# Layer 0's feed-forward network: up projection by a seven-product scheme, activations through DRAM, down projection as one stage

## The chip, the cores and the metric

One core of a Trainium2 chip runs the whole program; the other seven cores are idle. The metric is the device time of one execution in microseconds (us). PE is the matrix engine, PEld its weight loads, DVE the vector engine, ACT the scalar engine, POOL the GpSimd engine and SP the queue that issues nearly all transfers. L292 means line 292 of the kernel before; in rows of the changed kernel the numbers are those of its own file.

## The reference, cut to what matters

Two layers of a block; each has token mixers and then a feed-forward network. In layer 0 it runs over 768 tokens (512 of x, 256 of context), in layer 1 over the 512 of x. D is 1024, D_FF is 2816, all in float32.

```python
def dwconv3(x, w):                      # along tokens, x and context apart
    xp = jnp.pad(x, ((0, 0), (1, 1), (0, 0)))
    return xp[:, :-2] * w[0] + xp[:, 1:-1] * w[1] + xp[:, 2:] * w[2]

def conv_ffn(u, w_up, w_conv, w_down):
    a = dwconv3(u @ w_up, w_conv)       # w_up [1024, 5632]
    gate, val = jnp.split(a, 2, axis=-1)
    return (jax.nn.silu(gate) * val) @ w_down   # w_down [2816, 1024]

fx = conv_ffn(modulate(rmsnorm(x, g), shift, scale), ffn_up[l], ffn_conv[l], ffn_down[l])
x = x + mod_x[5] * rmsnorm(fx, norm_g[l, 3])
```

## The kernel before

**Numbers in two parts.** Each float32 factor is split into a high part that the matrix engine takes exactly and a low rest. A product is three passes: high by high, high by low, low by high. The input of the up projection lies in SBUF as UH and UL, features on the partitions. A weight tile is loaded (`load`, L262, on SP), ACT casts the high part (L255) and POOL subtracts it from the raw tile to get the low part (L256, `wl`, 128x1024). Both subtraction inputs lie in SBUF.

**Up projection of layer 0.** The 5632 columns are 22 pairs of 128-wide tiles, a gate tile f and a value tile f. `fm` (L305 and on) computes one tile for all 768 tokens: 8 k-tiles, three passes, and for each a matmul of 512 and one of 256 columns (L292), so 48 matmuls a tile and 96 a pair. The first pair goes through `fms`, which cuts the tokens into pieces of 256 and also computes the gate tile of pair 1.

**After a pair** (`up_pair`, L1286 and on) the three-tap convolution runs straight from PSUM: ACT scales the middle tap into `fcv` (L552), DVE adds the two others (L554, L557) for 512 and 256 tokens. Then ACT's Silu (L1298), DVE's product (L1299), ACT's high part `ah` (L1302) and DVE's low part `al` (L1303).

```python
    def dwconv(dst, src, w, hc):        # src is a place in PSUM
        ACT.activation(dst[:, 0:n], src[:, 0:n], AF.Copy, scale=w[1])
        for a, b in ((0, TX),) + (((TX, T),) if hc else ()):
            DVE.scalar_tensor_tensor(dst[:, a + 1 : b], src[:, a : b - 1], w[0], dst[:, a + 1 : b], ...)
            DVE.scalar_tensor_tensor(dst[:, a : b - 1], src[:, a + 1 : b], w[2], dst[:, a : b - 1], ...)
```

**Down projection of layer 0** (`ffn`, L1319 and on) is mixed in between: after each group of 2 to 5 pairs (`EDGES`), `down` (L1306; its products L1311) multiplies the group's activations with its rows of w_down for each of the six 128-token tiles j, and the result is added to y[j] in SBUF: ACT copies the first group (L1337), DVE adds the others from PSUM (L1339). In all 792 matmuls of 512 columns. The last group ends in `residual` (norm, gain, residual sum) and `to_u`, which transposes the result on PE into the input of layer 1.

**Beside it** `mod_dve` computes layer 1's six modulation vectors: w_mod comes in 512 KB pieces, DVE keeps a running sum `macc` (L416, L418; 128x512, all in SBUF), and ACT, POOL (L428, `ml`) and PE finish each half.

**What sets the order.** The program text is not the order of an engine: a scheduler lays the instructions of each engine out at build time by priorities and an estimate of durations. At run time each engine takes its own list strictly in that order and waits at its head. Tiles in PSUM (`mm` twice, `b2` once, two `b1`) and weight buffers (5 raw, 3 high) are given out in program order.

Of the kernel before, what the change touches and what calls it, by code (L numbers as in the profile page):

```python
# [44 lines left out]
def block_kernel(  # L45
# [412 lines left out]
    def mod_first(ch, hf, md):  # L458
        """Half of the columns of a chunk of layer 0, summed on DVE."""
# [19 lines left out]
    def mod_pe(ch, hf, md):  # L479
        """The same on PE."""  # L480
# [10 lines left out]
    def square(np_, ss, src):  # L491
        """ss = the mean square of src over the D features, or its part from these."""
# [10 lines left out]
    def to_u(np_, l, which, j0, xns, ks=range(KC)):  # L503
        """Modulate normalized token tiles j0, ... into the input of the next products."""
# [4 lines left out]
        for k in ks:  # L509
            ps = b1()  # L510
            for i, xn in enumerate(xns):
                PE.transpose(ps[:, i * P : (i + 1) * P], xn[:, k * P : (k + 1) * P], ident)
            tt = np_.tile([P, n], F32, tag="tt", name=nm("tt"), bufs=3)
            ACT.activation(
                tt, ps[:, 0:n], AF.Identity, scale=a[:, k, part : part + 1], bias=b[:, k, part : part + 1]
            )
            DVE.tensor_copy(UH[:, k, o : o + n], tt)  # L517
            DVE.tensor_sub(UL[:, k, o : o + n], tt, UH[:, k, o : o + n].bitcast(F32))  # L518
# [10 lines left out]
    def residual(np_, gs, j, y, src, v, dst, last):  # L529
        """v = x + mod * rmsnorm(y) for token tile j, stored; unless last, normalized again in place."""  # L530
# [30 lines left out]
    # ================= mLSTM gates =================  # L561
    def gate_prep(l, gp, cols):
# [32 lines left out]
        # rows 0-3: forward, in processing order (context, then x); rows 32-35: backward, reversed  # L595
# [31 lines left out]
        def natural(dst, src, fn):  # L627
            """dst (x then context, natural order) = fn(src) (processing order)."""
# [459 lines left out]
    def run(*gens):  # L1088
        """Round robin: (generator, steps per round)."""
# [16 lines left out]
    # ================= the layers =================  # L1106
# [5 lines left out]
    # first norm and first modulation  # L1112
# [51 lines left out]
    for l in range(2):  # L1164
# [62 lines left out]
        def rows(wr, w, k, bufs, eng=POOL):  # L1227
            raw, _ = load(w[k * P : (k + 1) * P, :].unsqueeze(1), 1)
            h = wr.tile([P, 1024], F32R, tag="wrh", name=nm("wrh"), bufs=bufs)
            lo = wr.tile([P, 1024], F32R, tag="wrl", name=nm("wrl"), bufs=bufs)  # L1230
            ACT.copy(h, raw)  # L1231
            eng.tensor_sub(lo, raw, h.bitcast(F32))  # L1232
            return h, lo

# [20 lines left out]
        y = [t(yb, [P, D], f"y{j}") for j in range(njs)]  # L1255
# [3 lines left out]
        for j in range(njs):  # L1259
# [14 lines left out]
            if j % 2:  # L1274
                late = to_u(np_, l, 1, j - 1, y[j - 1 : j + 1])
# [4 lines left out]
        if l == 1:  # L1280
            more_slots(raw=4)
# [37 lines left out]
        def ffn():  # L1319
            edges = EDGES[l]  # L1320
            pairs = [up_pair(0)]
            for g in range(len(edges) - 1):
# [4 lines left out]
                ws = [rows(wr, ffn_down[l], f, DOWN_ROWS[l]) for f in range(lo, hi)]  # L1327
# [15 lines left out]
        if l == 0:  # L1343
            pcs[1] = params(1, nc.sync)
            up = ffn()
            for _ in range(2):
                next(up)
            run((up, 1), (seq(*[mod_dve(1, ch, fp) for ch in (1, 0, 2, 4, 3, 5)]), 1))
        else:
            run((ffn(), 1))  # L1350
# [6 lines left out]
        for j in range(DOWN_AHEAD[l]):  # L1357
            pss.append(next(ring)())
            down(av, ws, j, pss[j], 0, len(av) - 1)
        for j in range(njs):  # L1360
            end = j == njs - 1
            if j < DOWN_AHEAD[l]:
# [8 lines left out]
            dst = x2d[j * P : (j + 1) * P, :] if l == 0 else out[0, j * P : (j + 1) * P, :]  # L1371
            residual(np_, gs, j, y[j], x1d[j * P : (j + 1) * P, :], y[j], dst, l == 1)
            if l == 0 and j % 2:
                late = to_u(np_, 1, 0, j - 1, y[j - 1 : j + 1])
        if l == 0:
            def ending(np_, yb, late):
                yield from late
                np_.release()
                yb.release()

            late = ending(np_, yb, late)
            wr.release()
            np_.release("gt0", "gt1", "xr", "sq")
            yb.release(*[f"y{j}" for j in range(4)])
            continue
# [84 lines left out]
```

## Time and profile before

| what | value |
|---|---|
| time of the 3 runs | median 2684.73 us (2673.37 to 2686.26) |
| profiled execution, first to last instruction | 2676.3 us (the page gives no other time of this execution) |
| median of the runs above that span | 8.4 us |
| mean granted clock of PE | 0.994 |
| chain of waits that ended last | PE 31% of the span, DVE 3%, all others under 2% |
| transfers | 297.96 MB, mean 111 GB/s |
| busiest lines on POOL | L256 637.0 us and L1232 118.0 us, both the low parts of weights |

Busy shares of an engine include the time in which it holds an instruction that cannot start yet. The mean over the span mixes stages, so the feed-forward stage of layer 0 is read by itself: its first product starts at 1022.4 us (L292 after the last w_out product) and the first product of layer 1 starts at 1605.6 us.

### The profile page before, as it was taken

What the parts mean: (1) busy time and instruction counts of PE and PEld (TensorE: products, weight loads), DVE (VectorE), ACT (ScalarE), POOL (GpSimd) and SP (SyncE); (2) the same over time, 40 slices, a digit from 0 to 9 for tenths busy, and PEclk for the clock granted to TensorE, in tenths of its full rate; (3) what the DMA queues carried; (4) which work ended last, traced back from release to release, by engine and by line L of the source; (5) the groups of instructions that cost most, each with busy time, mean ns of one, the idle gap of its engine ahead of it and who ended that gap; (6) DMA issues with size and microseconds to landing.
All of it is one profiled execution on the core that took longest, in us unless ns stands there. A gap on an engine that the chain in (4) does not pass through costs nothing. (4 is left out here: it accounts for less than half of the span.)

```text
span 2676.3 us, 35623 instructions
## 1 busy us (share of the span) xinstructions
PE 2583.5 (97%) x13859; PEld 2169.5 (81%) x13859; DVE 1449.0 (54%) x2510; ACT 992.0 (37%) x1663; POOL 896.2 (33%) x522
## 2 busy tenths in 40 slices
PE   6999999999999999999999999999999998999998
PEld 2887888888888878888888878787888876888886
DVE  6688784332462456477665565665434646523334
ACT  3454553222222234323322345555232333543332
POOL 3222223333232223233332333323343433444432
PEclk9999999999999999999999999999999999999999
DMA  6334353321331443233433342323433436433321
GB/s 230 91 110 126 104 162 117 113 79 56 106 96 57 132 138 120 88 110 119 134 119 102 121 137 84 109 82 117 126 103 101 120 96 189 150 95 95 99 67 55
DMA packets 321267, 297.96 MB, mean 111 GB/s; under 512 B 12532, under 2 KB 264252, under 8 KB 321100
## 3 DMA queue, kind: packets, MB, share of 16 engines
q1 hardware_dynamic: 320184, 294.11, 35.8%
q8 instruction: 110, 1.80, 0.3%
q10 hardware_dynamic: 916, 1.58, 0.2%
q14 instruction: 57, 0.47, 0.1%
HBM read 269.30 MB, written 26.35 MB: 110 GB/s over the span
## 5 line engine op out<-in xcount | busy, mean ns | idle before, releaser
L256 POOL TENSOR_TENSOR wl<-raw,wh 128x1024 fp32r<-128x1024 f32 x260 | 637.0, 2452 | 1198.6 <-ACT wh L255 1152.1
L292 PE MATMUL mm<-UH,wh 128*128 128x512 f32 (+1 forms) x2248 | 657.3, 352 | 6.8 <-DVE UH L517 4.6
L292 PE MATMUL mm<-UL,wh 128*128 128x512 f32 (+1 forms) x2248 | 645.3, 348 | 1.8 <-DVE UL L518 1.8
L255 ACT CAST wh<-raw 128x1024 fp32r<-128x1024 f32 x260 | 272.6, 1049 | 540.3 <-PE mm L292 363.0
L292 PE MATMUL mm<-UH,wl 128*128 128x512 f32 (+1 forms) x2248 | 451.6, 348 | 0.0
L292 PEld LDWEIGHTS mm<-UH,wh 128*128 128x128 f32 x2248 | 368.1, 189 | 63.7 <-DVE UH L517 5.7
L292 PEld LDWEIGHTS mm<-UL,wh 128*128 128x128 f32 x2248 | 366.5, 189 | 57.7 <-DVE UL L518 2.2
L292 PEld LDWEIGHTS mm<-UH,wl 128*128 128x128 f32 x2248 | 358.2, 189 | 56.3 <-issue 3.2
L418 DVE SCALAR_TENSOR_TENSOR macc<-mraw,sc,macc 128x512 f32<-128x512 f32 x224 | 206.4, 946 | 19.4 <-DMA mraw<-in_w_mod_dram 18.4
L1232 POOL TENSOR_TENSOR wrl<-raw,wrh 128x1024 fp32r<-128x1024 f32 x48 | 118.0, 2471 | 167.0 <-ACT wrh L1231 125.8
L292 PE MATMUL mm<-ys,wh 128*128 128x512 f32 (+1 forms) x768 | 166.0, 361 | 7.7 <-DVE bth L1020 7.1
L292 PEld LDWEIGHTS mm<-ys,wh 128*128 128x128 f32 x768 | 124.8, 188 | 30.2 <-issue 4.8
L554 DVE SCALAR_TENSOR_TENSOR fcv<-mm,fcol,fcv 128x511 f32<-128x511 f32 x89 | 58.3, 655 | 139.6 <-ACT fcv L552 139.5
L1231 ACT CAST wrh<-raw 128x1024 fp32r<-128x1024 f32 x60 | 62.7, 1050 | 140.7 <-DMA raw<-in_ffn_down_dram 63.9
L292 PE MATMUL mm<-U,wh 128*128 128x512 f32 (+1 forms) x496 | 111.2, 376 | 0.2 <-DVE y L536 0.2
L292 PEld LDWEIGHTS mm<-U,wh 128*128 128x128 f32 x496 | 89.2, 188 | 17.4 <-DVE y L536 0.4
L1020 DVE SCALAR_TENSOR_TENSOR bth<-bth,mm 128x768 f32<-128x768 f32 (+1 forms) x48 | 39.2, 817 | 115.6 <-PE mm L292 108.5
L1311 PE MATMUL mm<-wrh,ah 128*128 128x512 f32 x302 | 95.5, 393 | 1.2 <-DVE fcv L557 1.2
L1311 PE MATMUL mm<-wrl,ah 128*128 128x512 f32 x302 | 95.5, 393 | 0.0
L1311 PE MATMUL mm<-wrh,al 128*128 128x512 f32 x302 | 95.4, 392 | 0.0
L292 PE MATMUL mm<-ys,wl 128*128 128x512 f32 (+1 forms) x384 | 85.3, 357 | 0.0
L554 DVE SCALAR_TENSOR_TENSOR cv<-mm,pcol,cv 128x511 f32<-128x511 f32 (+1 forms) x28 | 17.7, 632 | 118.6 <-ACT cv L552 118.6
(306 smaller groups left out, 4116.2 us busy)
## 6 DMA issues: line engine op xcount, KB each, us to landing
raw<-in_w_in_dram SPq DMA_DIRECT2D x140, 512.0 KB
mraw<-in_w_mod_dram SPq DMA_DIRECT2D x88, 512.0 KB
raw<-in_ffn_up_dram SPq DMA_DIRECT2D x88, 512.0 KB
raw<-in_ffn_down_dram SPq DMA_DIRECT2D x44, 512.0 KB
raw<-in_w_branch_dram SPq DMA_DIRECT2D x32, 512.0 KB
gates<-bth SPq DMA_DIRECT2D x24, 384.0 KB
bth<-gates SPq DMA_DIRECT2D x24, 384.0 KB
raw<-in_w_out_dram SPq DMA_DIRECT2D x16, 512.0 KB
```

The source lines that it names most:

```text
L255: ACT.copy(h, raw)
L256: POOL.tensor_sub(lo, raw, h.bitcast(F32))
L292: PE.matmul(ps[:, c0:c1], lhsT=lw, rhs=r, start=s, stop=e)
L418: DVE.scalar_tensor_tensor(acc[v], mr[:, kk], sc[:, k, v : v + 1], acc[v], op0=ALU.mult, op1=ALU.add)
L554: DVE.scalar_tensor_tensor(dst[:, a + 1 : b], src[:, a : b - 1], w[0], dst[:, a + 1 : b], op0=ALU.mult, op1=ALU.add)
L1020: DVE.scalar_tensor_tensor(th[:, 0:n], th[:, 0:n], 1.0, pb[:, 0:n], op0=ALU.add, op1=ALU.mult)
L1231: ACT.copy(h, raw)
L1232: eng.tensor_sub(lo, raw, h.bitcast(F32))
L1311: PE.matmul(ps[:, h], lhsT=av[i][q][:, j * P : (j + 1) * P], rhs=ws[i][r][:, h], start=pi == 0 and i == 0, stop=pi == 2 and i == len(av) - 1,)
```

## The change

It touches layer 0's feed-forward network alone. Layer 1 keeps the old scheme.

- **Up by seven products.** Pairs 0 and 1 stay as they were in kind. For pairs 2 to 21 the product of [gate; value] weights with the input is taken as 2 by 2 blocks: gate and value tile are the two row blocks, the two halves of the 1024 features the inner blocks, tokens 0 to 383 and 384 to 767 the two column blocks. Strassen's scheme (Winograd's order of sums) needs seven block products instead of eight: 7 x 12 = 84 matmuls of 384 columns a pair.
- **Sums it needs.** Four sums of input blocks (T1 to T4) are made once on DVE and split into parts. Per pair, DVE makes the four half tiles `s12` and `s34` from the raw weights (128x512 each), and ACT and POOL split raw, s12, s34 and half of the value tile (`part`): three 128x1024 and one 128x512 subtraction on POOL.
- **Block results** come together in PSUM and, through ACT copies (`p1`, `u1`, `u2`) and three DVE sums of 384 columns, in SBUF tiles `gx` and `vx`. The convolution now reads these, not PSUM.
- **Activations** (`cv`) are stored to DRAM (`a_d`), 384 KB a pair, and read back in halves.
- **Down as a stage of its own** after the last pair: two sweeps of three token tiles, each summing all 22 f in PSUM (two `mm` and `b2`). w_down is loaded and split twice. The accumulation into y[j] is gone. The second sweep runs its last 4 f tile by tile.
- Layer 1's modulation vectors run at 0.4 steps per pair (chunks 1, 0) and per f of the down stage (2, 4, 3, 5). Weight buffers in this stage: 10 raw, 7 high.

```diff
+        def conv_act(f, gps, vps):
+            cg = fp.tile([P, T], F32, tag="cg", name=nm("cg"), bufs=1)
+            dwconv(cg, gps, [fc[:, 44 * i + f :][:, 0:1] for i in range(3)], True)
+            cv = fp.tile([P, T], F32, tag="cv", name=nm("cv"), bufs=2)
+            dwconv(cv, vps, [fc[:, 44 * i + 22 + f :][:, 0:1] for i in range(3)], True)
+            ACT.activation(cg, cg, AF.Silu)
+            DVE.tensor_mul(cv, cg, cv)
+            nc.sync.dma_start(a_d[f], cv)
+        def part(src, off, n=1024):
+            h = at("wh", [P, n], F32R, slot("wh"))
+            lo = at("wl", [P, n], F32R, off)
+            ACT.copy(h, src)
+            POOL.tensor_sub(lo, src, h.bitcast(F32))
+            return h, lo
+        def prepare(f):
...
+            DVE.tensor_add(s12[:, lo], r2[:, lo], r2[:, hi])
+            DVE.tensor_sub(s12[:, hi], s12[:, lo], r1[:, lo])
+            DVE.tensor_sub(s34[:, lo], r1[:, lo], r2[:, lo])
+            DVE.tensor_sub(s34[:, hi], r1[:, hi], s12[:, hi])
+            return part(r1, o1), part(s12, os12), part(s34, os34), (r2[:, hi], o2 + 2048, 512)
...
+        for j in range(3):
+            sl = slice(j * P, (j + 1) * P)
+            t1, t2, t3, t4 = (tf[:, :, sl] for tf in tfs)
+            DVE.tensor_sub(t1, blocks(j + 3, 0), blocks(j, 0))
+            DVE.tensor_sub(t2, blocks(j + 3, 4), t1)
+            DVE.tensor_sub(t4, blocks(j, 4), t2)
+            DVE.tensor_sub(t3, blocks(j + 3, 4), blocks(j + 3, 0))
+        for i in (1, 0, 2, 3):
+            ACT.copy(ths[i], tfs[i])
+            (DVE, POOL)[i % 2].tensor_sub(tls[i], tfs[i], ths[i].bitcast(F32))
...
+            product(b, w1, 0, "11", True, True)
+            ACT.copy(p1, b)
+            if pend:
+                pend.pop()()
+            w22 = part(*w22)
+            product(a, w1, 512, "21", True, True)
+            DVE.tensor_add(gx[:, 0:HT], a, p1)
+            product(b, w12, 512, "T2", False, True)
+            ACT.copy(u1, b)
+            product(c, w12, 0, "T1", True, True)
+            product(b, w34, 0, "T3", False, True)
+            ACT.copy(u2, b)
+            DVE.tensor_add(vx[:, HT:T], c, u2)
+            def rest():
+                product(b, w22, 0, "T4", False, True)
+                ACT.copy(vx[:, 0:HT], b)
+                product(c, w34, 512, "22", False, True)
+                DVE.tensor_add(gx[:, HT:T], c, u1)
+                conv_act(f, gx, vx)
...
+        run((ups(), 1), (seq(*[mod_dve(1, ch, mp) for ch in (1, 0)]), 0.4))
...
+            for s in range(2):
+                pss = [mm(), mm(), b2()]
+                last = NF - LAST_DOWN if s else NF
+                for f in range(last):
+                    w, a = factors(s, f)
+                    for i in range(3):
+                        down(pss[i], f, w, a, i)
...
+        run((sweeps(), 1), (seq(*[mod_dve(1, ch, mp) for ch in (2, 4, 3, 5)]), 0.4))
```

How the engines' lists change at the two places that matter most below.

DVE in the up stage of the kernel before, one pair: `fcv` is the convolution's tile, `b` and `mm` are places in PSUM, `fcol` the taps, `al` the low part of the activation.

```order
L554 SCALAR_TENSOR_TENSOR fcv_2672_11398<-b_2670_11349,fcol_8361,fcv_2672_11398 128x511
L557 SCALAR_TENSOR_TENSOR fcv_2672_11398<-b_2670_11349,fcol_8361,fcv_2672_11398 128x511
L554 SCALAR_TENSOR_TENSOR fcv_2672_11398<-b_2670_11349,fcol_8361,fcv_2672_11398 128x255
L557 SCALAR_TENSOR_TENSOR fcv_2672_11398<-b_2670_11349,fcol_8361,fcv_2672_11398 128x255
L554 SCALAR_TENSOR_TENSOR fcv_2678_11459<-mm_11410,fcol_8361,fcv_2678_11459 128x511
L557 SCALAR_TENSOR_TENSOR fcv_2678_11459<-mm_11410,fcol_8361,fcv_2678_11459 128x511
L554 SCALAR_TENSOR_TENSOR fcv_2678_11459<-mm_11410,fcol_8361,fcv_2678_11459 128x255
L557 SCALAR_TENSOR_TENSOR fcv_2678_11459<-mm_11410,fcol_8361,fcv_2678_11459 128x255
L1299 TENSOR_TENSOR fcv_2678_11459<-fcv_2672_11398,fcv_2678_11459 128x768
L1303 TENSOR_TENSOR al_2682_11468<-fcv_2678_11459,ah_2680_11467 128x768
```

The same place of the changed kernel, about half of a pair's rows (`b2` is the place in PSUM; `gx`, `vx`, `u1`, `u2`, `s12`, `s34`, `raw`, `macc` and `mraw` lie in SBUF):

```order
L1247 TENSOR_TENSOR vx_2481_2482_10233<-b2_2359_9702,u2_2477_2478_10231 128x384
L436 SCALAR_TENSOR_TENSOR macc_2734_2735_11525<-mraw_2796_2797_11815,sc_15_89,macc_2734_2735_11525 128x512
L1165 TENSOR_TENSOR s34_2529_10513<-raw_2526_10508,raw_2527_10510 128x512
L1166 TENSOR_TENSOR s34_2529_10513<-raw_2526_10508,s12_2528_10512 128x512
L576 SCALAR_TENSOR_TENSOR cv_2522_2523_10443<-vx_2481_2482_10233,fcol_2080_8362,cv_2522_2523_10443 128x511
L1253 TENSOR_TENSOR gx_2479_2480_10232<-b2_2359_9702,u1_2475_2476_10230 128x384
L579 SCALAR_TENSOR_TENSOR cv_2522_2523_10443<-vx_2481_2482_10233,fcol_2080_8362,cv_2522_2523_10443 128x511
L576 SCALAR_TENSOR_TENSOR cv_2522_2523_10443<-vx_2481_2482_10233,fcol_2080_8362,cv_2522_2523_10443 128x255
L436 SCALAR_TENSOR_TENSOR macc_2736_2737_11526<-mraw_2796_2797_11815,sc_15_89,macc_2736_2737_11526 128x512
L576 SCALAR_TENSOR_TENSOR cg_2520_2521_10437<-gx_2479_2480_10232,fcol_2080_8362,cg_2520_2521_10437 128x511
L576 SCALAR_TENSOR_TENSOR cg_2520_2521_10437<-gx_2479_2480_10232,fcol_2080_8362,cg_2520_2521_10437 128x255
L579 SCALAR_TENSOR_TENSOR cg_2520_2521_10437<-gx_2479_2480_10232,fcol_2080_8362,cg_2520_2521_10437 128x511
```

The eight convolution rows a pair now read SBUF (`vx`, `gx`), the four sums of weights are new, `al` has moved to the down stage, and the running sums of the modulation stand between them. From the first of the weights' sums to the last product `cv` DVE's list holds 88 + 88 convolution rows (511 and 255 columns), 22 products, 80 sums of 128x512, 60 sums of 128x384 from PSUM, and 82 rows of `macc`.

POOL in the up stage before (`wrl` is the low part of w_down, `ml` a step of the modulation):

```order
L256 TENSOR_TENSOR wl_10890<-raw_10887,wh_10889 128x1024
L428 TENSOR_TENSOR ml_10733<-macc_2541_10585,mh_10732 128x512
L428 TENSOR_TENSOR ml_10738<-macc_2543_10586,mh_10732 128x512
L1232 TENSOR_TENSOR wrl_2618_11044<-raw_11041,wrh_2616_11043 128x1024
L256 TENSOR_TENSOR wl_10951<-raw_10948,wh_10950 128x1024
```

And of the changed kernel, one pair and what follows it:

```order
L1152 TENSOR_TENSOR wl_2678_11183<-raw_2653_11102,wh_2677_11182 128x512
L1152 TENSOR_TENSOR wl_2657_11111<-raw_2652_11100,wh_2656_11110 128x1024
L1152 TENSOR_TENSOR wl_2659_11115<-s12_2654_11104,wh_2658_11114 128x1024
L1152 TENSOR_TENSOR wl_2661_11119<-s34_2655_11105,wh_2660_11118 128x1024
L446 TENSOR_TENSOR ml_3022_12798<-macc_2992_2993_12719,mh_3021_12797 128x512
```

Two subtractions of 128x1024 a pair (and one for w_down) have become three and a half, and w_down's 44 stand behind the last pair's. In the up stage POOL's list holds 60 of 128x1024, 20 of 128x512 and 11 `ml`.

## Rows read from the trace of the kernel before

**Rows 1.** The page, busy time of PE and PE's granted clock in 40 slices.

```profile
PE 2583.5 (97%) x13859; PEld 2169.5 (81%) x13859; DVE 1449.0 (54%) x2510; ACT 992.0 (37%) x1663; POOL 896.2 (33%) x522
PEclk9999999999999999999999999999999999999999
```

**Rows 2.** Busy time by stretch: us; PE, PEld, DVE, ACT, POOL; clock; DMA share, GB/s.

```profile
1022.40:1605.60 583.20, 575.03 (x3108) 488.66 (x3107) 370.56 (x471) 193.31 (x264) 201.21 (x108) 0.99 0.37 116
```

**Rows 3.** Timeline of PE, first rows of three up tiles (start, us, what).

```profile
1275.39 0.51 PE L292 MATMUL b<-UH,wh 128*128 128x512 f32 x2
...
1283.86 0.51 PE L292 MATMUL mm<-UH,wh 128*128 128x512 f32 x2
...
1292.34 0.51 PE L292 MATMUL mm<-UH,wh 128*128 128x512 f32 x2
```

**Rows 4.** Timeline of PE in a group of down products, 34 rows of two apart.

```profile
1259.05 0.61 PE L1311 MATMUL mm<-wrl,ah 128*128 128x512 f32 x2
...
1274.46 0.61 PE L1311 MATMUL mm<-wrh,al 128*128 128x512 f32 x2
```

**Rows 5.** Timeline of DVE and POOL, 1158 to 1176 us.

```profile
1158.40 2.40 POOL L256 TENSOR_TENSOR wl<-raw,wh 128x1024 fp32r<-128x1024 f32 x1 [0.47 <-ACT wh L255]
1158.79 0.47 DVE L554 SCALAR_TENSOR_TENSOR fcv<-b,fcol,fcv 128x255 f32<-128x255 f32 x1
1159.18 2.17 DVE L418 SCALAR_TENSOR_TENSOR macc<-mraw,sc,macc 128x512 f32<-128x512 f32 x1
...
1162.33 0.95 DVE L1299 TENSOR_TENSOR fcv<-fcv,fcv 128x768 f32<-128x768 f32 x1
1163.20 1.40 DVE L418 SCALAR_TENSOR_TENSOR macc<-mraw,sc,macc 128x512 f32<-128x512 f32 x2
...
1165.23 2.50 POOL L256 TENSOR_TENSOR wl<-raw,wh 128x1024 fp32r<-128x1024 f32 x1 [4.43 <-ACT wh L255]
1165.39 4.89 DVE L418 SCALAR_TENSOR_TENSOR macc<-mraw,sc,macc 128x512 f32<-128x512 f32 x4
...
1173.62 2.73 DVE L418 SCALAR_TENSOR_TENSOR macc<-mraw,sc,macc 128x512 f32<-128x512 f32 x4
```

**Rows 6.** The same, around 1181 us.

```profile
1178.57 2.53 POOL L428 TENSOR_TENSOR ml<-macc,mh 128x512 fp32r<-128x512 f32 x2
...
1181.03 3.24 DVE L1299 TENSOR_TENSOR fcv<-fcv,fcv 128x768 f32<-128x768 f32 x1
1181.05 2.42 POOL L1232 TENSOR_TENSOR wrl<-raw,wrh 128x1024 fp32r<-128x1024 f32 x1
```

**Rows 7.** One line's instructions: ns min/median/max, first and last start, forms.

```profile
L418 DVE SCALAR_TENSOR_TENSOR macc<-mraw,sc,macc x224: 728/744/2914, 121.5 to 1512.3; 128x512 f32<-128x512 f32 x112
...
L1299 DVE TENSOR_TENSOR fcv<-fcv,fcv x44: 692/957/3243, 1052.8 to 2646.1; 128x768 f32<-128x768 f32 x22, 128x512 f32<-128x512 f32 x22
...
L554 DVE SCALAR_TENSOR_TENSOR fcv<-mm,fcol,fcv x89: 461/749/752, 1047.3 to 2644.5; 128x511 f32<-128x511 f32 x59, 128x255 f32<-128x255 f32 x30
...
L554 DVE SCALAR_TENSOR_TENSOR zc<-z,pcol,zc x12: 478/748/959, 549.1 to 2049.1; 128x511 f32<-128x511 f32 x8, 128x255 f32<-128x255 f32 x4
...
L256 POOL TENSOR_TENSOR wl<-raw,wh x260: 2350/2401/3941, 27.5 to 2626.8; 128x1024 fp32r<-128x1024 f32 x130
```

**Rows 8.** Timeline of DVE, two sums of 128x512 in a row.

```profile
1566.88 1.28 DVE L536 TENSOR_TENSOR y<-y,gt 128x512 f32<-128x512 f32 x2
```

**Rows 9.** DVE's sums of 384 columns from PSUM: busy us, mean ns | idle.

```profile
L893 DVE TENSOR_TENSOR E<-b,E 128x384 f32<-128x384 f32 x24 | 12.0, 550 | 9.0 <-PE b L883 9.0
```

**Rows 10.** Timeline of PE at a stall in the layer's last residuals.

```profile
1576.07 0.61 PE L1311 MATMUL b<-wrh,ah 128*128 128x512 f32 x2
1579.24 0.44 PE L512 MATMUL b<-ident,y 128*128 128x128 f32 x2 [2.56 <-ACT y L546]
...
1582.01 1.05 PE L1311 MATMUL b<-wrl,ah 128*128 128x512 f32 x2
```

**Rows 11.** Busy time by stretch of 10 us around that stall, columns as rows 2.

```profile
1570.00:1580.00 10.00, 6.92 (x33) 5.12 (x32) 5.33 (x9) 6.04 (x17) 3.09 (x6) 1.00 0.41 158
1580.00:1590.00 10.00, 10.00 (x44) 8.12 (x43) 8.68 (x22) 6.46 (x16) 2.28 (x4) 0.83 0.52 148
1590.00:1600.00 10.00, 8.11 (x35) 6.20 (x34) 6.82 (x12) 6.35 (x17) 3.10 (x6) 0.88 0.60 223
```

More of the change, by code (lines that the diff above doesn't have):

```diff
@@ L192, in more_slots, with __init__, back @@
             slots["raw"].append(arena.base + 4 * arena.take(1024)[0])
+    class Lent:
+        def __init__(self, **counts):
+            self.got = []
+            for kind, n in counts.items():
+                for _ in range(n):
+                    piece = arena.take(1024)
+                    off = arena.base + 4 * piece[0]
+                    slots[kind].insert(0, off)
+                    self.got.append((kind, off, piece))
+        def back(self):
+            for kind, off, piece in self.got:
+                slots[kind].remove(off)
+                arena.give(*piece)
     ps_ = {"mm": 2, "b2": 1, "b1": 2, "pool": tc.alloc_tile_pool(name="psum", bufs=1, space=PSUM)}
@@ L501, in rstd, with to_u @@
         return r
-    def to_u(np_, l, which, j0, xns, ks=range(KC)):
+    def to_u(np_, l, which, j0, xns, ks=range(KC), inplace=None):
         part = 0 if j0 < 4 else 1
@@ L512, in to_u @@
                 PE.transpose(ps[:, i * P : (i + 1) * P], xn[:, k * P : (k + 1) * P], ident)
[L513 to L518, printed above, removed]
+            src, uh, ul = ps[:, 0:n], UH[:, k, o : o + n], UL[:, k, o : o + n]
+            if inplace is None:
+                tt = np_.tile([P, n], F32, tag="tt", name=nm("tt"), bufs=3)
+            else:
+                tt = inplace[:, j0 : j0 + len(xns), k * P : (k + 1) * P]
+                src, uh, ul = (z.rearrange("p (j t) -> p j t", t=P) for z in (src, uh, ul))
+            ACT.activation(tt, src, AF.Identity, scale=a[:, k, part : part + 1], bias=b[:, k, part : part + 1])
+            DVE.tensor_copy(uh, tt)
+            DVE.tensor_sub(ul, tt, uh.bitcast(F32))
             yield
@@ L1107, in xsrc, with make_rows, rows @@
+    def make_rows():
+        def rows(wr, w, k, bufs, eng=POOL):
+            raw, _ = load(w[k * P : (k + 1) * P, :].unsqueeze(1), 1)
+            h = wr.tile([P, 1024], F32R, tag="wrh", name=nm("wrh"), bufs=bufs)
+            lo = wr.tile([P, 1024], F32R, tag="wrl", name=nm("wrl"), bufs=bufs)
+            ACT.copy(h, raw)
+            eng.tensor_sub(lo, raw, h.bitcast(F32))
+            return h, lo
+        return rows
     def xsrc(l, j):
@@ L1225, in block_kernel @@
         wr = Pool()
[L1227 to L1233, printed above, removed]
+        rows = make_rows()
         fc = conv_params(l)
@@ L1254, in block_kernel @@
         yb = Pool()
-        y = [t(yb, [P, D], f"y{j}") for j in range(njs)]
+        if hc:
+            Y = t(yb, [P, NT * D], "Y").rearrange("p (j d) -> p j d", j=NT)
+            y = [Y[:, j] for j in range(NT)]
+        else:
+            y = [t(yb, [P, D], f"y{j}") for j in range(njs)]
         np_ = Pool()
@@ L1274, in block_kernel @@
             if j % 2:
-                late = to_u(np_, l, 1, j - 1, y[j - 1 : j + 1])
+                late = to_u(np_, l, 1, j - 1, y[j - 1 : j + 1], inplace=Y if hc else None)
         wr.release()
@@ L1279, in block_kernel @@
         fp = Pool()
-        if l == 1:
-            more_slots(raw=4)
+        if hc:
+            pcs[1] = params(1, nc.sync)
+            late = fast_ffn(fc, Y, late, yb, np_, wr, fp)
+            continue
+        more_slots(raw=4)
         ring = cycle((mm, mm, b2))
@@ L1326, in ffn @@
                     yield
-                ws = [rows(wr, ffn_down[l], f, DOWN_ROWS[l]) for f in range(lo, hi)]
+                ws = [rows(wr, ffn_down[l], f, DOWN_ROWS) for f in range(lo, hi)]
                 if hi < NF:
@@ L1341, in ffn @@
             ffn.last = (pairs[lo:hi], ws)
[L1343 to L1350, printed above, removed]
+        run((ffn(), 1))
         fp.release()
@@ L1356, in block_kernel @@
         pss = []
-        for j in range(DOWN_AHEAD[l]):
+        for j in range(DOWN_AHEAD):
             pss.append(next(ring)())
@@ L1370, in block_kernel @@
                 DVE.tensor_add(y[j][:, h], pss[j][:, h], y[j][:, h])
[L1371 to L1385, printed above, removed]
+            residual(np_, gs, j, y[j], x1d[j * P : (j + 1) * P, :], y[j], out[0, j * P : (j + 1) * P, :], True)
         np_.release()
```

143 lines of the change are left out of this document (138 added, 5 removed).

## The prediction, made before the changed kernel ran

> **What bounds the kernel now.** First the page: PE is busy for 97% of the span, and its granted clock stands at 9 tenths or more in all 40 slices [rows 1]. A mean over the span can hide stages, so next the one stage that changes, from its first up product to layer 1's first: 583.2 us, of which PE is busy 575.03, at a clock of 0.99, DVE 370.56, POOL 201.21, and transfers run at 116 GB/s [rows 2]. So PE bounds this stage, with 8 us idle, and fewer columns would help it if nothing else becomes later. Third the timeline of PE for the price of a product: an up tile starts every 8.48 us (1275.39, 1283.86, 1292.34) [rows 3], a pair every 16.95, and 34 steps of two down products take 15.41 us, 0.4533 each [rows 4]. Fourth, since the change hands work to DVE and POOL, their own timelines, read for what one does to the other.
>
> Those show **a wait that no engine's share tells**. Four running sums of 128x512 on DVE take 2.73 us by themselves; with a POOL subtraction of 2.50 us beside them, 4.89 [rows 5]. A product of 128x768 takes 0.95, and 3.24 beside a POOL subtraction of 2.42 [rows 5, 6]. The line's statistics agree: median 744 ns and longest 2914 for the sums, 957 and 3243 for the product. But the convolution that reads PSUM is never longer than 752 ns over 89 instructions [rows 7]. So a DVE instruction with only SBUF operands stands still while POOL subtracts: it lost 2.16 us to 2.50 of POOL and 2.29 to 2.42. One that reads PSUM doesn't. Before, most of DVE's work in the pairs read PSUM.
>
> **The change, part by part.**
>
> *PE, up.* Two matmuls of 512 and 256 columns take 8.48 / 24 = 0.353 us, two of 512 take 0.4533 [rows 3, 4]: 0.392 ns a column and 0.026 us an instruction, so one of 384 is an estimated 0.1766 us. 84 of them are 14.83 us a pair where 96 took 16.95. Over 20 pairs: 297 for 339, **-42 us, if PE is fed**.
>
> *POOL.* Per pair three subtractions of 128x1024 at 2.40 (median 2401 ns) [rows 7], one of 512 columns at about 1.2, and 11 / 20 of an `ml` at 1.26 [rows 6]: 9.1 us. Alone it fits in 14.83.
>
> *DVE.* Issue intervals, since instructions overlap at their ends: of `macc` (2.73 - 1.40) / 2 = 0.66, of the convolution's 255 columns 1159.18 - 1158.79 = 0.39, of the product 1163.20 - 1162.33 = 0.87 [rows 5]; a 512 sum, 1.28 for two [rows 8], with the same overlap of 0.08, 0.60; a PSUM sum of 384 lasts 0.550 [rows 9], so 0.47. The convolution from SBUF is priced as from PSUM: `zc`, which reads SBUF, has the median 748 [rows 7]. A pair then needs 4 x 0.66 + 4 x 0.40 = 4.24 for the convolution, 0.87 for the product, 4 x 0.60 = 2.40 for s12 and s34, 3 x 0.47 = 1.41 for sums from PSUM, and 82 / 20 x 0.66 = 2.71 for `macc`: **11.6 us**. That would fit too.
>
> *The two together.* All of DVE's work but 1.41 us now has only SBUF operands, so POOL's time is added to it rather than laid beside it. With 2.2 us lost per subtraction of 1024 (between the 2.16 and 2.29 above), half of it for the 512, and 0.55 x 1.1 for `ml`: 6.6 + 1.1 + 0.6 = 8.3, less 0.2 that falls on PSUM sums, 8.1. So DVE needs 11.6 + 8.1 = **19.7 us a pair**: more than PE's 14.83, and more than the 16.95 of before. 20 pairs: 394 for 339, **+55 us**. Bounds: POOL's subtractions at their least (2.35) [rows 7] and each hand-over overlapped, 3 x 2.35 + 1.2 + 0.7 of POOL and 10.2 of DVE's SBUF work less 0.7 give 18.4, +29; if each subtraction also waits for a running DVE instruction (half of 0.66) and DVE for 0.1 more, 3.55 x 0.43 more, 21.2, +85.
>
> What queues behind it: DVE takes its list in order, so behind a blocked `cv`, `s34` or `macc` stand the three sums that empty halves of `b2`. PE's next product into that half waits for them, and so does ACT's copy of the next block. s12 and s34 of pair f+2 also stand there; their splits on ACT and POOL come later with them. Nothing that PE does can hide this, since every pair needs the same again. SP loads some four pairs ahead, so the loads are costed at nothing; behind the `a_d` store in SP's queue stand loads of weights, and that cover is four pairs deep.
>
> *Start and tail.* Before pair 2, DVE must make T1 to T4 (twelve sums) and two low parts, and POOL two more; PE meanwhile has pairs 0 and 1. By the same prices DVE is done some 4 us after PE: +4. The last pair's convolution lies under the first down products: -7.
>
> *Down stage.* 792 matmuls as before, 0.2266 each, 179.5 us: nothing on PE. Per f of a sweep DVE and POOL need some 3.5 us (one w_down subtraction at 2.4, one half `al`, `macc`) against PE's 18 x 0.2266 = 4.08, so they keep up. Loads are 44 w_down tiles, 44 halves and the modulation, 48 MB in 185 us, some 260 GB/s; before, 223 GB/s took a share of 0.60 [rows 11], which makes 372 at a share of 1. Costed at nothing; with no better use than that row the bound is +30. The way through DRAM needs the last `cv` to come back: +2. Between the sweeps three PSUM tiles must be emptied by residuals: +4, bounded by 0 and by three stalls of 2.56 [rows 10]. What the stage held beside its products, 583.2 - 22 x 16.95 - 179.5 = 31 us [rows 2 to 4], are transposes, the modulation's products and the 8 us of idle; I take 6 of it, with bounds of 0 and 12, as falling into PE's new idle time: -6. The accumulation into y[j] (DVE) leaves the path of no one.
>
> Sum: 55 + 4 - 7 + 2 + 4 - 6 = **+52 us**. The profiled execution's span of 2676.3 becomes 2728; the median of the runs is 8.4 above that span, so the forecast is **2736 us**.
>
> **The skill against the rows.** The Trainium skill (SBUF — State Buffer, "Who interferes with whom") says that a DVE instruction with two SBUF inputs contends with a GpSimd instruction that reads SBUF, and that the loser is blocked for the whole instruction. Which rows wait agrees with it; in size the rows say 2.16 of 2.50, and by whole instructions a pair would cost some 0.8 us more, about 2752.
>
> **Rivals.**
> *A, the forecast:* shared port, 19 to 21 us a pair, 2722 to 2762. For it: [rows 5 to 7] and the lists of DVE and POOL. Chance 0.62.
> *B, the same but packed:* 17.6 to 18.9 us a pair, because POOL works while DVE reads PSUM or waits: +10 to +36, 2695 to 2720. Against it: only 1.41 us a pair read PSUM. 0.16.
> *C, the lock plus waits that nothing covers, and PE's clock:* after a 2.56-us stall [rows 10] the clock was 0.83 in the next 10 us [rows 11], 1.7 us lost. With PE idle a quarter of each pair this can come every pair: 14.83 + 1.7 = 16.5 is still under 19.7, but where the lost time falls behind a late DVE result it is added, as is an engine that waits for another twice in a loop. 21.5 to 23.5 a pair, 2773 to 2813. 0.13.
> The Trainium skill (TensorE: Matmul & The Clock Gate, "HAM oscillation — how this bites in real kernels") describes a kernel whose PE waits in every tile and then runs at 1.2 GHz after each wait; the one stall above agrees, and no row shows it repeated.
> *D, the other side, faster:* PE still bounds the stage, at 14.83 a pair: 297 for 339, with 6 us of start and sweeps, -36: 2649. It decides at 16.65 us a pair of DVE and POOL: there, with those 6 us, the time is that of before. It needs POOL's subtractions to cost DVE under 1.4 us each; the rows say 2.16 and more. 0.05.
> *E, the down stage bound by transfers:* 48 MB at 223 GB/s [rows 11] is 215 us, +30 on top of A: 2766. 0.04.
> That the change doesn't cut the products can be left out: PE's list holds 1680 matmuls of 384 columns.
>
> **How the numbers follow.** The likeliest is A, 2736. The range goes from B's foot, 2695, to 2790, within C: what lies outside is D, C's upper half and a rest, about 0.15. A measurement of this kernel can tell about 0.5%, 13.4 us, from no change: faster than that is D, 0.05; same is B's lower edge and D near its turning point, 0.05; slower 0.90.
>
> **What would show it.** Right: PE's first up product of a pair every 19 to 21 us; PE's idle time before up products ended by DVE or by ACT and POOL behind it, some 5 us a pair; the convolution's 511 rows, 752 at most before, now over 2000 ns wherever POOL runs, while sums from `b2` stay near 550; PE's clock below 1 in the up stage; a down stage near 185 us. Wrong: pairs every 15 us with DVE's rows at 750 (D), convolution rows that aren't longer beside POOL (then the price of the shared port is not this), or a down stage much above 190 with DMA as the releaser (E).

## The result, and the profile after

The changed kernel takes 2849.03 us (median of four runs, 2848.52 to 2851.42) against 2684.72: a ratio of 1.0627, 95% interval 1.0604 to 1.0649, **164 us slower**. The forecast was 2736 in a range of 2695 to 2790. The direction was right, the size three times too small. (Of the profiled executions, the one of the changed kernel spans 2849.7 us and ran for 2851.42; the one of before, 2676.3, was some 7 us quicker than the median of its kernel, so the spans differ by 173.4.)

The page of the changed kernel, the same two lines as [rows 1]:

```profile
PE 2610.0 (92%) x13595; PEld 2221.0 (78%) x13595; DVE 1629.1 (57%) x2649; ACT 1091.0 (38%) x1829; POOL 1054.3 (37%) x586
...
PEclk8999999999999998888888999999999999999999
```

Seven slices in the middle, where the stage lies, are below 9. Busy time by stretch (us; PE, PEld, DVE, ACT, POOL; clock; DMA share, GB/s), pairs 2 to 21 and then the down stage, which answer to [rows 2] (from pair 2's first product at 1076.8 to the last up product's end at 1566.4, and from there to the last down product's end at 1779.2):

```profile
1076.80:1566.40 489.60, 364.30 (x1726) 342.56 (x1727) 369.28 (x401) 174.77 (x241) 214.91 (x94) 0.86 0.29 93
1566.40:1779.20 212.80, 194.79 (x840) 156.30 (x838) 128.90 (x137) 87.18 (x145) 117.16 (x65) 0.96 0.66 216
```

A pair takes 489.6 / 20 = 24.5 us. No engine fills that time: PE is busy for 74% of it, at a clock of 0.86, DVE for 75%, POOL for 44%. A resource that bounds a stage would be near 100%; this picture is that of engines that take turns.

Where the 173.4 us of span went. Before, the stage of [rows 2] has 37.5 us from its first up product (1022.47) to the first of pair 2 (1059.97), 339 for 20 pairs by the price of [rows 3], and the rest. After, the first up product starts at 1028.3. The forecast's start (+4) stands in the second line, its tail, way through DRAM, sweeps' boundary and idle time (-7, +2, +4, -6) in the third.

| part | before | forecast | after | forecast was short by |
|---|---|---|---|---|
| pairs 2 to 21 | 339 | 394 | 489.6 | 96 |
| first up product to pair 2 | 37.5 | 41.5 | 48.5 | 7 |
| rest of the stage, down products among it | 206.7 | 199.7 | 212.8 | 13 |
| outside the stage, where nothing was changed | 2093 | 2093 | 2099 | 6 |

The waits of PE in pairs 2 to 21 of the changed kernel (us in total, times, longest):

```profile
PE mm L1217 <- DVE gx L1241: 66.8, 19, 6.9
PE b L1217 <- DVE gx L1253: 46.9, 19, 4.8
```

Twice in nearly every pair PE stands still for one of DVE's sums of 384 columns: 113.7 us. DVE and POOL wait in their turn, DVE for ACT's copy of a block that PE has just finished, POOL for DVE's rows that make `s34` (`s` here), since its low part takes the place of the raw weights that they read:

```profile
DVE vx L1247 <- ACT u L1246: 78.7, 19, 6.4
```

```profile
POOL wl L1152 <- DVE s L1165: 112.4, 9, 14.7
```

One turn of this ring (each engine waits for another, and the last for the first) in the timeline of all engines (start, us, what, idle time before and what ended it):

```profile
1477.47 4.91 DVE L579 SCALAR_TENSOR_TENSOR cv<-vx,fcol,cv 128x511 f32<-128x511 f32 x2
...
1482.31 1.13 DVE L576 SCALAR_TENSOR_TENSOR cg<-gx,fcol,cg 128x511 f32<-128x511 f32 x2
...
1485.03 0.54 DVE L1241 TENSOR_TENSOR gx<-mm,p 128x384 f32<-128x384 f32 x1
...
1485.62 0.47 PE L1217 MATMUL mm<-th,wh 128*128 128x384 f32 x1 [2.68 <-DVE gx L1241]
...
1493.04 0.56 DVE L1247 TENSOR_TENSOR vx<-b,u 128x384 f32<-128x384 f32 x1 [6.00 <-ACT u L1246]
...
1495.47 0.69 DVE L1165 TENSOR_TENSOR s<-raw,raw 128x512 f32<-128x512 f32 x1 [1.88 <-PE mm L1217]
...
1496.30 4.38 POOL L1152 TENSOR_TENSOR wl<-raw,wh 128x512 fp32r<-128x512 f32 x2 [14.19 <-DVE s L1165]
...
1496.96 4.00 DVE L576 SCALAR_TENSOR_TENSOR cv<-vx,fcol,cv 128x511 f32<-128x511 f32 x2 [0.19 <-ACT cv L574]
...
1500.88 0.54 DVE L1253 TENSOR_TENSOR gx<-b,u 128x384 f32<-128x384 f32 x1
...
1501.48 0.44 PE L1217 MATMUL b<-th,wh 128*128 128x384 f32 x1 [2.75 <-DVE gx L1253]
```

Follow it: POOL starts when DVE's L1165 is done (1496.16); its subtractions hold DVE's convolution rows (4.00 us for two rows that took 1.13 at 1482.31, when POOL was idle); the sum L1253 stands behind them in DVE's list; PE waits for the sum. PE's next products feed `u2`, for which DVE then waits, 6.00 us in this turn. The shared port that the forecast rests on is there, in the statistics of the lines (ns min/median/max):

```profile
L576 DVE SCALAR_TENSOR_TENSOR cv<-vx,fcol,cv x44: 472/2555/2898, 1068.6 to 1570.5; 128x511 f32<-128x511 f32 x22, 128x255 f32<-128x255 f32 x22
...
L1253 DVE TENSOR_TENSOR gx<-b,u x20: 543/544/548, 1113.5 to 1567.7; 128x384 f32<-128x384 f32 x20
```

The convolution's longest row was 752 ns from PSUM [rows 7] and is 2898 from SBUF; the sum L1253 from PSUM is never longer than 548. Which rows wait is what the Trainium skill says (SBUF — State Buffer, "Who interferes with whom").

**The wait that nobody had to have.** Why does PE wait for these two sums at all? The list of waits in the built program answers it (`DVE_49` is the counter of DVE's finished instructions). T1 of the next pair writes one half of `b2`, columns 512 to 895:

```
L1217 MATMUL b_2359_9702<-th_2309_2310_9504,wh_11390 128x384 [waits DVE_49]
```

and the count of DVE that it waits for is that of L1253, which reads columns 0 to 383: the other half, of the pair before. T2 likewise waits for L1241 of its own pair, which reads the half `a` of `mm`, while T2 adds to the half `b`; in DVE's list L1241 stands behind convolution rows of the pair before. No data passes between them. Two block results in one tile are taken as one thing by the layer that places the waits.

### The profile page after: what moved, and what is told of

Same layout as the page of the kernel before. It is cut to its first block, busy times and chain, and to the rows that moved or that the text cites. A ratio compares the mean times of both kernels' runs of the same rounds, so it can differ in the third digit from the quotient of the medians.

```text
span 2849.7 us, 35848 instructions
## 1 busy us (share of the span) xinstructions
PE 2610.0 (92%) x13595; PEld 2221.0 (78%) x13595; DVE 1629.1 (57%) x2649; ACT 1091.0 (38%) x1829; POOL 1054.3 (37%) x586
## 5 line engine op out<-in xcount | busy, mean ns | idle before, releaser
L310 PE MATMUL mm<-UH,wh 128*128 128x512 f32 (+1 forms) x1832 | 550.0, 355 | 7.4 <-DVE UH L539 5.7
L310 PE MATMUL mm<-UL,wh 128*128 128x512 f32 (+1 forms) x1832 | 539.7, 351 | 2.0 <-DVE UL L540 2.0
L310 PE MATMUL mm<-UH,wl 128*128 128x512 f32 (+1 forms) x1832 | 376.2, 351 | 0.0
L310 PEld LDWEIGHTS mm<-UH,wh 128*128 128x128 f32 x1832 | 304.1, 189 | 53.5 <-DVE UH L539 6.9
L310 PEld LDWEIGHTS mm<-UL,wh 128*128 128x128 f32 x1832 | 303.4, 189 | 48.6 <-DVE UL L540 2.5
L436 DVE SCALAR_TENSOR_TENSOR macc<-mraw,sc,macc 128x512 f32<-128x512 f32 x224 | 212.8, 975 | 28.6 <-DMA mraw<-in_w_mod_dram 27.2
L1152 POOL TENSOR_TENSOR wl<-raw,wh 128x1024 fp32r<-128x1024 f32 (+1 forms) x40 | 87.3, 2199 | 195.3 <-DVE s L1165 112.4
L1217 PE MATMUL mm<-th,wh 128*128 128x384 f32 x240 | 95.9, 399 | 68.2 <-DVE gx L1241 66.8
L1152 POOL TENSOR_TENSOR wl<-s,wh 128x1024 fp32r<-128x1024 f32 x40 | 107.3, 2701 | 0.0
L576 DVE SCALAR_TENSOR_TENSOR cv<-vx,fcol,cv 128x511 f32<-128x511 f32 (+1 forms) x44 | 87.9, 2020 | 9.0 <-ACT cv L574 8.9
L1217 PE MATMUL mm<-tl,wh 128*128 128x384 f32 x240 | 91.8, 382 | 0.0
```

Of the source, the lines that this page charges most:

```text
L310: PE.matmul(ps[:, c0:c1], lhsT=lw, rhs=r, start=s, stop=e)
L436: DVE.scalar_tensor_tensor(acc[v], mr[:, kk], sc[:, k, v : v + 1], acc[v], op0=ALU.mult, op1=ALU.add)
L1152: POOL.tensor_sub(lo, src, h.bitcast(F32))
L1217: PE.matmul(ps, lhsT=w[r][:, o + k * P : o + (k + 1) * P], rhs=B[b][q][:, k], start=start and i == 0, stop=stop and i == 11, skip_group_ch ...
```

## The experiments

Two theories: **L**, the port that DVE and POOL share sets 24.5 us a pair by itself; **W**, the waits for the other half of a PSUM tile close a ring around it. The runs stand in the order in which they ran; a scheduler gives each its own order, so an edit may move other instructions a little.

**1. PSUM tiles of their own.**

```diff
-            X = mm()
-            a, b, c = X[:, 0:HT], X[:, 512 : 512 + HT], cs[:, 512 * (f % 2) :][:, 0:HT]
+            a, b, c = (pst(q, 512)[:, 0:HT] for q in ("qa", "qb", "qc"))
```

(The PSUM pool is given up before pair 2 and after pair 21 and taken anew with other tiles.)

> The seven block results of a pair get PSUM tiles of their own (two each of a, b and c) where the change had halves of shared tiles; nothing else is edited. Theory W (false waits): in the changed kernel PE's products T2 and T1 wait for DVE's sums of the other half of the same tile (66.8 and 46.9 us), which closes a ring between PE, DVE and POOL; with own tiles both waits go, and the pair falls from 24.5 us to what DVE and POOL together need, some 19 to 20: 2740 to 2770 us in all. Theory L (the shared port of DVE and POOL alone sets 24.5 us a pair): within 15 us of the 2849 of the change.

2780.06 us, ratio to the kernel before 1.0376 (1.0353 to 1.0400): 69 us less than the change, by one edit that changes no arithmetic, and 10 above the range of theory W. No wait of PE for DVE's sums is left. Its pairs 2 to 21, and PE's longest wait there:

```profile
1079.60:1481.70 402.10, 328.82 (x1705) 315.75 (x1705) 352.80 (x372) 162.53 (x232) 209.24 (x90) 0.92 0.31 97
```

```profile
PE qb L1217 <- ACT u L1246: 57.9, 18, 6.7
```

A pair takes 20.1 us, and DVE is busy for 88% of it: what the forecast had as 19.7. L by itself has fallen. DVE still makes PE wait, but through ACT's list: the copy `u2` stands there behind the Silu, which waits for a convolution row.

```profile
1292.92 0.84 ACT L1143 ACTIVATE cg<-cg 128x768 f32<-128x768 f32 x1 [9.02 <-DVE cg L579]
...
1294.61 0.47 ACT L1246 COPY u<-qb 128x384 f32<-128x384 f32 x1
...
1295.13 0.69 PE L1217 MATMUL qb<-th,wh 128*128 128x384 f32 x1 [6.65 <-ACT u L1246]
```

**2. No subtraction on POOL, tiles as in the change**, and **3. neither.**

```diff
             ACT.copy(h, src)
-            POOL.tensor_sub(lo, src, h.bitcast(F32))
-            return h, lo
+            return h, h
```

> The changed kernel without POOL's subtractions for pairs 2 to 21 (the low part of these weights is left out; PE reads the high part in its place, so that it has as many products). Theory L: without POOL's 3.55 subtractions a pair nothing blocks DVE, which then needs 11.6 us a pair; with the ring of theory W still closed the pair becomes 24.5 - 8.1 = 16.4 to 18, 2690 to 2720 us. If the port is not in the ring (the ring is PE, ACT and DVE by themselves): above 2810.

> Both edits (own PSUM tiles; low parts of the weights of pairs 2 to 21 left out). If false waits and the shared port are the whole of it, PE bounds the stage at 14.8 to 15.5 us a pair with its clock back at 1: 2849 - 20 x 9.3 = 2663, 2650 to 2680 us. If something third holds it (the clock, loads, ACT): above 2700.

2685.09 us, 5 below the range of theory L, and 2667.6 us, one run each. Pairs 2 to 21 of the first, and PE's waits there for the same sum:

```profile
1065.90:1402.30 336.40, 316.30 (x1726) 297.50 (x1726) 241.00 (x397) 167.06 (x240) 29.15 (x18) 0.98 0.44 136
```

```profile
PE mm L1215 <- DVE gx L1239: 14.3, 14, 7.7
```

and of the second:

```profile
1071.50:1373.80 302.30, 299.38 (x1705) 296.19 (x1705) 225.08 (x367) 163.76 (x231) 25.73 (x15) 0.99 0.41 131
```

With both causes gone a pair takes 15.1 us, the 14.83 of the forecast's PE term and some of the modulation's products. Us a pair in the four cases:

| | POOL subtracts | no POOL subtraction |
|---|---|---|
| halves of shared tiles | 24.5 (the change) | 16.8 |
| own tiles | 20.1 | 15.1 |

The subtractions on POOL cost 5.0 or 7.7, the false waits 1.7 or 4.4: each is dearer beside the other, by 2.7. W holds, but as a second cause; the port is the larger one. That it is the port, and not that low parts come late from POOL, is seen in DVE's rows and in that no wait of PE in pairs 2 to 21 of the change or of run 1 names POOL. The price of a subtraction can be read too: between runs 1 and 3 DVE's busy time falls from 352.8 to 225.1 us, 127.7 over 20 x 3.5 subtractions of 1024, some 1.8 us each.

**4. The down half of the change alone**: plain pairs 1 to 21 with the convolution from PSUM.

```diff
...
+        ring = cycle((mm, mm, b2))
...
+        def ups():
+            for f in range(1, NF):
+                conv_act(f, *[fm(0, ffn_up[0], q * DFF + f * P, True, lambda: next(ring)()) for q in range(2)])
+                yield
```

> The changed kernel's storing to DRAM and its down stage of its own, with the plain up products of before in all 22 pairs (48 x 512 and 48 x 256 columns a pair, convolution from PSUM). It shows what the down half of the change costs alone. If the down stage itself costs its 209 us against 180 of products, some 20 us more than before: 2695 to 2715 us. If its slowness comes from what the up stage leaves behind: 2665 to 2690.

2709.55 us, one run: some 28 us more than before. Its up stage and its down stage:

```profile
1028.10:1410.50 382.40, 380.96 (x2211) 330.76 (x2210) 194.44 (x291) 126.97 (x151) 134.94 (x62) 1.00 0.40 123
1410.50:1632.40 221.90, 200.16 (x851) 159.49 (x851) 153.37 (x150) 86.02 (x145) 118.19 (x67) 0.94 0.66 219
```

The up stage is PE's alone, at a clock of 1.00. The down stage takes 222 us where its products need 180, at 0.94: its slowness is its own and doesn't come from the up stage. The 20 pairs from pair 2 on take 344.5 us here (1066.1 to the first down product at 1410.6) and 302.3 in run 3: the forecast's 42 us for seven products instead of eight, once PE is fed. That the two whole times differ by 42 us too is partly luck, since start, stage ends and the executions outside the stage differ as well.

**5. Own tiles, low parts on DVE.** The subtraction in `part` is `DVE.tensor_sub`.

> As the run with own PSUM tiles, and the low parts of the weights of pairs 2 to 21 are subtracted by DVE and not by POOL: 4.2 us more work a pair for DVE (3.55 x 1.18, after the 1.76 us of a 128x1536 subtraction), 8.5 us less for POOL. Theory P (the shared port makes a POOL subtraction cost DVE 2.2 us, more than its own 1.18): DVE needs 11.6 + 4.2 = 15.8 us a pair against the 20.1 measured with own PSUM tiles, 2780 - 20 x 4.2 = 2696, 2680 to 2710 us. Rival Q (DVE at 88 per cent busy is simply full, port or not): 4.2 us a pair more, about 2860 us.

2680.46 us, ratio 0.9998 (0.9988 to 1.0007), at the foot of theory P's range: the whole loss is gone, with DVE doing more work. Its pairs 2 to 21:

```profile
1074.40:1388.00 313.60, 302.67 (x1709) 297.51 (x1709) 303.43 (x447) 166.20 (x233) 28.82 (x15) 0.98 0.40 125
```

15.7 us a pair, for P's 15.8. DVE gained 303.4 - 225.1 = 78.3 us over run 3, 1.12 a subtraction of 1024, where the same subtraction on POOL cost it some 1.8 by standing still. Q has fallen. A wait that runs 1 and 3 had too (6.7 and 8.2 us) stands at the stage's end, where the PSUM pool is given up: the first down product waits for the last use of the pool.

```profile
PE mm L1292 <- DVE mod L395: 7.4, 1, 7.4
```

**6. The convolution of pairs 0 and 1 from PSUM** (`conv_act(0, *pss)` ahead of the T sums, pair 1's gate tile in `b2`).

> As the run before, and the convolution of pairs 0 and 1 reads PSUM as in the kernel before (no copies to gx and vx), with the gate tile of pair 1 in b2, so that pair 0's convolution stands ahead of the T sums on DVE. If PE's waits at the start (9.89 and 10.23 us in the changed kernel) come from those copies and the DVE work behind them: 8 to 18 us less than the run before. If they come from T1 to T4 and their low parts alone: within 5 us of it.

2684.12 us, ratio 1.0010 (1.0000 to 1.0020): no gain, and within the 5 us of the second theory. PE's wait for ACT's copy of `vx` (9.5 us) became one of 10.0 for a convolution row; run 8 shows that T1 to T4 were not its reason either.

**7. Less modulation in the up stage.**

```diff
-        run((ups(), 1), (seq(*[mod_dve(1, ch, mp) for ch in (1, 0)]), 0.4))
+        run((ups(), 1), (seq(*[mod_dve(1, ch, mp) for ch in (1,)]), 0.2))
...
-        run((sweeps(), 1), (seq(*[mod_dve(1, ch, mp) for ch in (2, 4, 3, 5)]), 0.4))
+        run((sweeps(), 1), (seq(*[mod_dve(1, ch, mp) for ch in (0, 2, 4, 3, 5)]), 0.5))
```

> As the run before, and one vector of the modulation in the up stage (0.2 steps a pair) where two were, five in the down stage (0.5 steps per f). If DVE's own work bounds the up stage still (15.8 us a pair with 2.7 of macc, against 14.83 of PE): some 0.5 to 1 us a pair less, 10 to 20 us, of which the down stage gives back what its DVE and its loads lack, 0 to 10. If PE bounds the up stage already: 0 to 10 us slower.

2693.79 us, ratio 1.0042 (1.0027 to 1.0057). A pair falls to 15.1, as expected where DVE bounds it, but the down stage gives back 24 us (239.9 for 215.9), more than twice what was allowed for, so that the whole is 10 us slower than run 6.

**8. Own tiles without giving up the pool.**

```diff
-            a, b, c = (pst(q, 512)[:, 0:HT] for q in ("qa", "qb", "qc"))
+            a, b, c = cs[:, 512 * (f % 2) :][:, 0:HT], mm()[:, 0:HT], b1()[:, 0:HT]
```

> As the run with low parts on DVE and the early convolution, but the own tiles come from the places that were there (b from mm, c from b1, a from the halves of b2), so that the PSUM pool isn't given up and taken anew before the down stage. That pool change held the first down product for 7.4 us and the first product of pair 2 for 10. If both go and nothing takes their place: 2681 - 15 = 2666, 2660 to 2674 us, faster than the kernel before by 0.3 to 0.8 per cent. If DVE, busy all through the start, is what these waits were about: 2676 to 2684.

2676.72 us, ratio 0.9988 (0.9976 to 1.0000): by the time, the second theory's range, though the waits went as the first had it. The waits of 7.4 and 10.0 us are gone, and pair 2 begins 38.0 us after the first up product (48.2 in run 6). But in the down stage another has grown:

```profile
PE b L411 <- DVE gc L407: 9.4, 1, 9.4
```

a transposition for a gain vector, placed in PE's list before DVE had its input.

**9. Sweep ends apart, gain later.** The first sweep too does its last four f tile by tile; that transposition is issued a step later.

> As the run before, and two edits in the down stage: the first sweep too runs its last four f tile by tile, so that its three residuals end apart, and the transposition of a gain vector is issued one step later. In the runs so far PE stands still for 3.5 + 1.9 us at the sweeps' boundary (products waiting for the residuals to empty PSUM), 3.6 at the transposes behind it, 5.6 at the gain, each with a stretch at half clock behind it. If the boundary is the reason for the down stage's 215 us against 180 of products: 8 to 14 us less than the run before, about 2655. If loads (250 to 267 GB/s there) are: within 4 us of it.

2673.54 us, ratio 0.9972 (0.9960 to 0.9983), the **fastest version that leaves nothing out, 0.3% under the kernel before**. By the medians it gave 3 us over the run before, not 8 to 14, and the two intervals overlap. Its down stage:

```profile
1379.80:1593.60 213.80, 198.22 (x848) 158.59 (x848) 155.37 (x154) 81.89 (x136) 117.03 (x62) 0.94 0.69 232
```

The waits moved on: 5.7 us for a residual, 4.1 at a transpose and 4.1 at another right behind the last down product, 3.8 at the gain.

**10. Modulation swapped**: vectors 2, 4, 3, 5 beside the pairs, 1 and 0 in the first sweep.

> As the run before, but the modulation vectors of one accumulator (2, 4, 3, 5: sixteen loads of 512 KB twice over) stand in the up stage and the two of two accumulators (1, 0) in the first sweep; DVE's work moves little, 8 MB of loads move from the down stage (0.6 to 0.8 of the transfer time) to the up stage (0.4). If PE's late gain products (3.8 to 9.4 us, held by DVE, which waits 20 to 27 us for loads of w_mod) and the half-clock stretches behind them come from these loads: 6 to 14 us less, about 2663. If the down stage's loads cost nothing: 2670 to 2680.

2695.80 us, ratio 1.0054 (1.0035 to 1.0073). Slower, against the expectation. Its pairs and its down stage:

```profile
1066.80:1398.30 331.50, 309.91 (x1732) 301.23 (x1730) 312.15 (x462) 170.65 (x239) 39.45 (x14) 0.97 0.46 144
1403.70:1622.70 219.00, 197.62 (x842) 157.30 (x843) 138.36 (x152) 86.32 (x143) 119.32 (x67) 0.94 0.58 192
```

The loads did move (192 GB/s for 232 in the down stage), and the down stage became no shorter (219.0 for 213.8 us). But its two sweeps went opposite ways. First and second sweep of run 9, then of run 10:

```profile
1379.80:1482.60 102.80, 97.23 (x412) 78.11 (x413) 71.57 (x73) 37.91 (x63) 54.05 (x27) 0.95 0.73 246
1482.50:1593.50 111.00, 101.00 (x438) 80.59 (x436) 83.85 (x82) 44.08 (x74) 62.98 (x36) 0.94 0.66 219
```

```profile
1403.70:1522.60 118.90, 102.96 (x429) 79.84 (x430) 94.17 (x100) 43.62 (x71) 61.99 (x31) 0.91 0.61 203
1522.50:1622.70 100.20, 94.77 (x415) 77.56 (x414) 44.19 (x52) 42.70 (x72) 57.42 (x37) 0.97 0.54 178
```

The second sweep, now without modulation, is 11 us shorter; the first, which has all of it, is 16 us longer, with fewer GB/s (203 for 246) but DVE busy for 94.2 us in place of 71.6, and PE waiting 12.4 us for the modulation's `mh` of ACT. So the modulation beside a sweep costs it time; whether by its loads or by its work, this run doesn't tell. The pairs lost 16 us, with PE's products of the modulation waiting for POOL's `ml` (12.2 us).

## Why the prediction was right and wrong

- **PE's own term, right.** 14.83 us a pair forecast; 15.1 with PE fed (run 3), and the 42 us shown between the pairs of runs 4 and 3.
- **The shared port, right in kind, a sixth too dear.** 2.2 us a subtraction forecast, some 1.8 measured. The sum of 19.7 us a pair was met by 20.1 (run 1), partly by luck: DVE's busy time was 17.6, and 2.5 us of idle stood in place of the rest.
- **The step that failed** is "behind a blocked cv, s34 or macc stand the three sums that empty halves of b2. PE's next product into that half waits for them". PE's next product waits for the sum of the *other* half as well, and the same in `mm` (one of the three sums, L1241, empties a half of `mm` and not of `b2`). I took the halves as separate places because the code uses them so, and put this wait at nothing beside DVE's 19.7 us. It makes PE wait twice in each pair for a sum that stands in DVE's list behind rows of the pair before, and turns a late DVE into a ring: 4.4 us a pair, 87 of the 96 us that this term was short. With this wait alone taken away, the pairs take 20.1 us and the time, 2780 (run 1), lies inside the stated range.
- **Rival C** had the shape ("an engine that waits for another twice in a loop"), but without its place, and with 0.13 and 21.5 to 23.5 us a pair it stood below the 24.5 measured. Its other half, the clock, came true: 0.86 in the stage. In the turn shown above PE's products follow each other in 0.32 us from 1480.43, after a stall of 2.75 before 1477.61, and in 0.17 from 1489.37: the levels 1.2 and 2.4 GHz, with a granted clock of 0.50 and 1.00 (rows below). PE was busy for 364.3 us in the change and for 299.4 in run 3, in which it hardly waits, for as many block products: so the lower clock cost some 65 us of PE time, beside 125 us of idle. That agrees with what the Trainium skill says of a kernel that waits in every tile (TensorE: Matmul & The Clock Gate, "HAM oscillation — how this bites in real kernels"); here the waits are for DVE, not for a transfer.

```profile
1477.61 0.44 PE L1217 MATMUL b<-th,wh 128*128 128x384 f32 x1 [2.75 <-DVE gx L1253]
...
1480.43 0.52 PE L1217 MATMUL mm<-UH,wh 128*128 128x384 f32 x1
1480.75 0.52 PE L1217 MATMUL mm<-UL,wh 128*128 128x384 f32 x1
...
1489.37 0.34 PE L1217 MATMUL mm<-UH,wh 128*128 128x384 f32 x1
1489.55 0.33 PE L1217 MATMUL mm<-UL,wh 128*128 128x384 f32 x1
```

```profile
1479.10:1482.40 3.30, 3.30 (x13) 3.29 (x12) 3.30 (x3) 0.00 (x0) 3.01 (x2) 0.50 0.00 0
1489.40:1502.90 13.50, 10.76 (x61) 10.22 (x60) 7.79 (x7) 5.87 (x9) 6.60 (x3) 1.00 0.27 79
```

- **Start**, 4 us forecast, 11 measured: PE waits 9.9 us ahead of pair 2 for an ACT copy (`gx`, L1175) that frees a place in PSUM, and 10.2 more for the copy `p1` inside the 489.6. In run 8, in which the convolution of pairs 0 and 1 reads PSUM and no pool is taken anew, pair 2 begins 38.0 us after the first up product, for 37.5 before, though DVE has more to do: so the amount of DVE's work alone doesn't make this wait. Run 6 has the first of the two edits without the second and keeps a wait of 10.0; the second alone was not run.
- **Rest of the stage**, 7 us less than before forecast, 6 more measured. Of PE's waits there, 18 us in all, 6.1 are for the activations read back and 5.5 for residuals at the sweeps' boundary, where the forecast had 2 and 4; 5.0 stand at a transposition that had no term, 1.5 at the modulation, and the clock is 0.96. The -7 and the -6 are not to be seen. No wait of PE there names a transfer, which the forecast gave as rival E's sign, but run 10 doesn't settle what the loads cost.
- **Rival D** (faster) would have decided at 16.65 us a pair of DVE and POOL. Run 5 gets under it, 15.7, but its gain of 25 us in the pairs is eaten by start and down stage, so that it only draws level.

Open: why the layer that places the waits takes both halves as one was not looked into; that it does is read from the list and from run 1. What makes the down stage 209 to 222 us long against 180 of products in the runs with the same modulation, and how much of its waits could be scheduled away, wasn't settled by runs 9 and 10.

## What to carry to other kernels

A subtraction moved to POOL is not free because POOL is idle: where DVE's operands all lie in SBUF, 128x1024 on POOL cost DVE some 1.8 us and on DVE 1.12. Two results in the halves of one PSUM tile can wait for each other; read the built program's list of waits against what the data needs, before the run. Saving an eighth of the products only pays where the sums that it asks for keep up with PE, since PE pays for each late one twice, in the wait and in the clock behind it.

## What the runs showed that I had not expected

- Two causes that cost 1.7 and 5.0 us a pair alone cost 9.4 together: an engine's lateness is passed on only where somebody waits for it.
- Giving up a PSUM pool and taking it anew held the first product behind it for 7.4 us (run 5), until the last use of any of its tiles, a 128x16 row of DVE.
- With nothing on POOL in the way, DVE was busy for 97% of the pairs of run 5 (303.43 of 313.60 us) and PE too (302.67): two engines near full can go side by side when neither holds the other.
